# Residual rows of the last group in four parts, and the feed-forward tail's products in another order

## The chip, the core and the metric

The kernel runs on one core of a Trainium2 chip. The core has five engines with a queue each: TensorE (PE in the profile; its weight loads are PEld), VectorE (DVE), ScalarE (ACT), GpSimd (POOL) and SyncE (SP), which here issues most of the DMAs. The metric is the device time of one execution in microseconds (us); the time of a version is the median of its runs.

## What is computed

One decoder layer for 2048 tokens of width 1024 in float32. The reference, cut to what matters here:

```python
a = _rmsnorm(h, g_pre_mix)
u = a @ W_in                       # conv value, conv gate, q, k, v
conv_out = _conformer_conv(...)    # GLU, causal depthwise conv, LayerNorm, swish
attn_out = _stick_breaking(...)    # 8 heads of 64
y = concat(conv_out, attn_out) @ W_out
h = x + _rmsnorm(y, g_post_mix)
f_in = _rmsnorm(h, g_pre_ffn)
f = (silu(f_in @ w_gate) * (f_in @ w_up)) @ w_down      # D_FF = 2816
out = h + _rmsnorm(f, g_post_ffn)
```

## The kernel before

Tokens are worked in four groups of 512 (`g` 0 to 3), each of four row tiles of 128. Float32 matmuls are made of three: each operand is split into a high part `H` (ACT) and a rest `L` (DVE or POOL), and `L*H`, `H*H` and `H*L` are added in PSUM. So every product below is 12 matmuls of 128x128 by 128x512.

The feed-forward part works on two pairs of groups, (0, 1) and (2, 3), and computes gate and up of a pair by seven products in place of eight (a Winograd scheme): the weight matrices and the inputs are cut into 2x2 blocks and summed first. P1 and P2 (function `c11`) and, for the first pair, P4 (function `p4`) are computed earlier, beside attention, and stored in DRAM. Weight sums come from `sums` and lie in DRAM in pairs, two to a tile of 512 KB. The function `part` writes one half of such a tile.

What is left is the stage of the function `five`: 44 blocks, 22 for the first pair of groups, 22 for the second; in each pair of groups 11 column blocks `j`, gate (`i` = 0) and then up (`i` = 1). A block of the first half has the products P5, P7, P6 and P3, one of the second half also P4. PSUM tile `b2` takes P6, then P7 on top (and P4 on top of that); `b3` takes P5, then P3 on top. DVE makes the results of them:

- `u2 = b2 + s1` after P6 (`s1` is P1, loaded; method `second`),
- `u3 = b2 + s1` after P7, then in the first half `p4_ = u3 + p4_`, then `u3 = b3 + u3` after P5,
- `b3 = b3 + u2` after P3.

`result` makes of each of the four the `silu` (gate, on ACT, into a tile of `u`) or the product with the gate's (up, on DVE). After an up block `hidden` makes four sums for the down product (`s1`, `s2`, `a21`, `s4`) and puts the stores of the seven tiles on the list `late`, which `flush` empties two at a time after a product.

Order: products and the sums made through `dve` are kept in the order in which they are written (`tc.keep_in_program_order`). All else (splits, loads, residual rows, input sums) is put by a scheduler that runs when the program is built, and may move as its buffers and inputs allow. The written order in a round of the loop is: P5 of block n; what is left `behind` from block n-1 (a result, `hidden`, and the work of `todo`); P7 of block n; `u3`, `p4_`, `u3`; the split of the first weight pair of block n+1; P6 of block n+1; `u2` of block n+1; P4 of block n (second half); the split of the second weight pair; P3 of block n; `b3`.

`weights` loads for a block: `a22` (tag `row`, 4 buffers) with the stored P4 or a raw weight, the pair (6, 5) in a tile of tag `raw`, and the pair (7, 3) in a tile `raw2` of tag `row`. They are split into `wH` and `wL`, three buffers each.

`todo` gives each block its share of other work, one or two steps of the generator `steps`: first the residual rows of the last group (`residual_parts`, a load `xr` of the row of x, the mean square on ACT with its output in `junk`, `rs` on POOL, a product with the gain on DVE, two adds on POOL, the store to `hd`, a second mean square, a scaling on ACT), then the input sums of the second pair (`input_sums`, transposes of those rows, DVE and POOL sums, stores), then the loads of two of its operands (`operands`). `xr` and `junk` are tiles of tag `row` too. `residual_parts` stops twice; a step does the second part of a row after the first of the next.

The operands are held in slots: `x2` (products 6 and 5 of the first half), `e4`/`e5` (7), `e0`/`e1` (3); `e2`/`e3` get operand 4 of the second half, when the input sums are made. At the end of block 21 operands 7 and 3 are loaded anew for the second half.

After `five` come the down products (in the profile `dps`), in order of product and column block; the change touches them only through the stores of `late`.

## Time and profile before

| | us |
|---|---|
| median of 3 runs | 2599.94 |
| lowest and highest run | 2595.02, 2601.57 |
| the profiled execution, its own time | 2596.21 |
| its span, first to last instruction | 2594.5 |

The mean granted TensorE clock of the profiled execution is 0.977 of full speed. Its stages near the change: the last group's attention and output projection end at 1541.9 us; `five` runs from there to 2151.2; the down products to the end.

In the rows of the profile, L1072 is the line of `dve`, L760 that of the feed-forward matmuls, L1064 and L1065 those of the weight splits, L808 a split of an operand, L1053 the load of a weight pair, L722 the residual's product on DVE, L725 its adds on POOL, L192 the root for `rs`. `b` stands for any PSUM tile of the stage. The buffers of `u2` and `u3` are called `cy`, `cs` and `glu`; `glu` names those of `s1` as well. `accf` is the three sums for down, `a` the tile with `p4_`, `sumf`, `rbf`, `lng` and `accf` are also the tiles of `u`. Of the operands, `xH__17525` is that of P6, `xH__17543` of P5, `e__17561` of P7 and `e__17579` of P3. A row of a timeline gives the start and length in us, the engine, line, operation, what is written from what, the shape, how many in a row, and in brackets how long the engine was idle before and what ended that.

### The profile page before, as it was taken

How to read it: one execution, taken by the hardware profiler on the slowest of the kernel's cores; microseconds unless marked ns; L12 is line 12 of the kernel's file. 1: busy time of each engine (PE TensorE's matmuls, PEld its weight loads, DVE VectorE, ACT ScalarE, POOL GpSimd, SP SyncE). 2: the span in 40 equal slices, each digit the busy share in tenths (PEclk: the TensorE clock that was granted, in tenths of full speed). 3: DMA queues.
4: the chain of work that ended last, by engine and by line, in shares of the span. 5: the costliest groups of instructions: out<-in, count | busy, mean ns of one | idle time of the engine just before them, and what ended most of it. 6: DMA issues, size and time to landing. Idle time of an engine off the chain costs nothing. (4 is left out here: it accounts for less than half of the span.)

```text
span 2594.5 us, 35632 instructions
## 1 busy us (share of the span) xinstructions
PE 2434.6 (94%) x11156; PEld 1963.6 (76%) x11156; DVE 1788.6 (69%) x2321; ACT 1292.8 (50%) x2398; POOL 1473.1 (57%) x1844
## 2 busy tenths in 40 slices
PE   7989989998999999999999988899999999999997
PEld 6877767776777777887788766777777777887886
DVE  5797589958996898876544545766555655557556
ACT  4555555555555656667756734332332233453543
POOL 5764678556755777559433226764443444567556
PEclk9999999999999999999999989999999999999999
DMA  9989888988898898747977636986656557668655
GB/s 341 326 302 310 287 260 279 348 268 284 286 314 272 321 345 280 270 152 235 306 247 235 221 108 220 323 291 223 199 190 201 192 197 262 193 192 283 206 189 174
DMA packets 289182, 657.31 MB, mean 253 GB/s; under 512 B 33889, under 2 KB 42081, under 8 KB 288993
## 3 DMA queue, kind: packets, MB, share of 16 engines
q1 hardware_dynamic: 264704, 622.01, 71.6%
q10 hardware_dynamic: 24288, 33.04, 3.5%
q8 instruction: 88, 1.44, 0.2%
q14 instruction: 102, 0.83, 0.1%
HBM read 460.92 MB, written 193.99 MB: 252 GB/s over the span
## 5 line engine op out<-in xcount | busy, mean ns | idle before, releaser
L573 POOL TENSOR_TENSOR A<-A,om 128x512 f32<-128x512 f32 (+2 forms) x320 | 312.6, 977 | 410.0 <-DVE om L572 372.0
L572 DVE TENSOR_TENSOR_SCAN om<-om,one,z 128x513 f32<-128x513 f32 (+2 forms) x320 | 351.7, 1114 | 110.0 <-ACT A L570 104.5
L1065 POOL TENSOR_TENSOR wL<-raw,wH 128x512 fp32r<-128x512 f32 x176 | 248.9, 1441 | 286.5 <-issue 158.2
L476 DVE SCALAR_TENSOR_TENSOR cv<-glu,cw,cv 128x512 f32<-128x512 f32 x464 | 347.4, 749 | 6.7
L1245 DVE TENSOR_TENSOR xL__21999<-t__22001,xH__21998 128x512 fp32r<-128x512 f32 x154 | 199.1, 1301 | 159.6 <-ACT xH__21998 L1244 159.4
L1243 POOL TENSOR_TENSOR xL__21997<-t__22000,xH__21996 128x512 fp32r<-128x512 f32 x154 | 207.6, 1353 | 175.0 <-ACT xH__21996 L1242 174.5
L256 PE MATMUL inps<-xH,wL 128*128 128x512 f32 x640 | 260.8, 408 | 11.3 <-ACT sg L422 10.3
L249 DVE TENSOR_TENSOR TL<-at,TH 128x512 fp32r<-128x512 f32 (+1 forms) x320 | 188.8, 600 | 112.0 <-ACT TH L248 111.6
L260 PE MATMUL inps<-xL,wH 128*128 128x512 f32 x640 | 258.6, 405 | 0.2 <-DVE xL L392 0.2
L258 PE MATMUL inps<-xH,wH 128*128 128x512 f32 x640 | 258.2, 404 | 0.0
L760 PE MATMUL dps<-xH__21996,xL__21999 128*128 128x512 f32 x616 | 240.9, 391 | 8.1 <-DVE xL__21999 L1245 7.2
L568 ACT ACTIVATE om<-z 128x512 f32<-128x512 f32 (+2 forms) x320 | 171.6, 539 | 153.5 <-PE z L563 70.6
L760 PE MATMUL dps<-xL__21997,xH__21998 128*128 128x512 f32 x616 | 240.8, 391 | 2.0 <-POOL xL__21997 L1243 2.0
L760 PE MATMUL dps<-xH__21996,xH__21998 128*128 128x512 f32 x616 | 240.5, 390 | 0.0
L844 POOL TENSOR_TENSOR sum<-sum 128x512 f32<-128x512 f32 x132 | 172.6, 1308 | 84.8 <-DMA sum<-in_w_up_dram 28.5
L248 ACT ACTIVATE TH<-at 128x512 fp32r<-128x512 f32 (+1 forms) x320 | 168.0, 547 | 103.2 <-PE at L589 94.0
L1242 ACT ACTIVATE xH__21996<-t__22000 128x512 fp32r<-128x512 f32 x154 | 97.2, 631 | 233.0 <-POOL xL__21997 L1243 148.7
L589 PE MATMUL at<-idr,A 128*128 128x128 f32 x1088 | 191.4, 280 | 7.5 <-POOL A L573 5.6
L210 ACT ACTIVATE wH<-raw 128x1024 fp32r<-128x1024 f32 x156 | 165.6, 1064 | 65.0 <-DMA raw<-in_w_in_dram 29.6
L1064 ACT ACTIVATE wH<-raw 128x512 fp32r<-128x512 f32 x176 | 101.1, 623 | 165.0 <-PE b L760 76.4
L570 ACT ACTIVATE A<-z 128x512 f32<-128x512 f32 (+2 forms) x320 | 168.6, 542 | 19.2 <-PE at L589 14.4
L589 PEld LDWEIGHTS at<-idr,A 128*128 128x128 f32 x1088 | 142.2, 144 | 43.9 <-POOL A L573 6.8
(294 smaller groups left out, 6225.8 us busy)
## 6 DMA issues: line engine op xcount, KB each, us to landing
wL<-wL SPq DMA_DIRECT2D x156, 512.0 KB, 5.1
raw<-in_w_in_dram SPq DMA_DIRECT2D x80, 512.0 KB, 6.4
t__22001<-u SPq DMA_DIRECT2D x154, 256.0 KB, 2.8
c<-c ACTq DMA_DIRECT2D x88, 256.0 KB, 4.4
t__22000<-wd SPq DMA_DIRECT2D x88, 256.0 KB, 2.9
K<-kd SPq DMA_DIRECT2D x80, 256.0 KB, 4.7
V<-vd SPq DMA_DIRECT2D x80, 256.0 KB, 4.7
u<-accf SPq DMA_DIRECT2D x22, 768.0 KB, 4.1
```

What stands on the lines that cost most here:

```text
L249: nc.vector.tensor_tensor(L, ps, H.bitcast(F32), ALU.subtract)
L256: nc.tensor.matmul(ps, WL[:, kc], aH[t](k), start=k == 0, stop=False)
L258: nc.tensor.matmul(ps, WH[:, kc], aH[t](k), start=False, stop=False)
L260: nc.tensor.matmul(ps, WH[:, kc], aL[t](k), start=False, stop=k == KT - 1)
L476: nc.vector.scalar_tensor_tensor(to, gl[c][:, k:k + G], cw[:, c, k:k + 1], a, ALU.mult, ALU.add))
L572: nc.vector.tensor_tensor_scan(r, r, z[:, 0:1].to_broadcast([P, w + 1]), one, ALU.mult, ALU.bypass)
L573: nc.gpsimd.tensor_tensor(a[:, 0:w], a[:, 0:w], om[:, G - w + 1:G + 1], ALU.mult)
L589: nc.tensor.transpose(pt[:, j * P:(j + 1) * P], u["A"][j][:, b * P:(b + 1) * P], id32)
L760: return nc.tensor.matmul(ps, a, b, skip_group_check=True, **flags)
L1065: nc.gpsimd.tensor_tensor(l, t, f32(h), sub)
L1243: nc.gpsimd.tensor_tensor(WL, w, f32(WH), sub)
L1245: nc.vector.tensor_tensor(UL, t, f32(UH), sub)
```

## The change

`residual_parts` is given its row and junk tiles. For the last group the rows of x lie in the slots `e2` and `e3`, and the squares go to a tile of tag `ev` (bf16); the other groups use tag `row` as before. It stops three times more finely: after the first mean square, after the adds, after the store with the second mean square, and at the end. A step does one part of up to four rows, the oldest first, so that a row's parts come one block apart. There are seven such steps in place of five, and `todo` gives block 16 two steps.

The weight pairs are (6, 7) and (5, 3), in the stores of `sums` and in `weights`.

In the round of a block P7 comes first and then P5. `u3 = b2 + s1` and the p4 sum are written after P5 as they were after P7. `hidden` stops after two sums: the first two stay in `behind`, with the stores of two tiles, and the other two are made in the next block between the p4 sum and `u3 = b3 + u3`.

```diff
-    def residual(T, keep=False):
-
-        for _ in residual_parts(T, keep):
+    def residual(T):
+
+        for _ in residual_parts(T, row("xr"), row("junk")):
             pass
 
-    def residual_parts(T, keep):
+    def residual_parts(T, r, junk=None, keep=False):
+
         g, t = divmod(T, TT)
         if t == 0:
             gpo.append(gain(g_post_mix))
         y = ys[g][t]
-        r, junk = row("xr"), row("junk")
         nc.sync.dma_start(r, x[T * P:(T + 1) * P, :])
         rs = sp.tile([P, 1], F32, tag="rs", name="rs", bufs=4)
         rms_of(rs, y, junk)
...
             nc.gpsimd.tensor_tensor(y[:, es], y[:, es], r[:, es], ALU.add)
+        yield
         nc.sync.dma_start(hd[T], y)
         rms_of(rstd2[:, T:T + 1], y, junk)
         done.add(("h", T))
+        yield
         if keep:
...
-                    ns = (6, 5) if m in (6, 5) else (7, 3)
+                    ns = (6, 7) if m in (6, 7) else (5, 3)
...
-            for ns in ((6, 5), (7, 3)):
+            for ns in ((6, 7), (5, 3)):
...
             dve(s1, a21, a22, add)
             dve(s2, s1, a11, sub)
+            for n, t in ((1, a11), (4, a22)):
+                late.append([1, t, "u", g, n, j])
+            yield
             dve(a21, a21, a11, sub)
             dve(s4, a12, s2, sub)
-            for n, t in ((1, a11), (4, a22), (7, a21), (2, a12)):
+            for n, t in ((7, a21), (2, a12)):
                 late.append([1, t, "u", g, n, j])
             late.append([1, sums3, "u3", g, j])
+            yield
...
             behind = []
+            more_h = []
             for n in range(NB):
                 b3 = gu("b3")
-                b.mul(b3, 5, True)
+                b.mul(b.b2, 7, False)
                 nxt = Block(n + 1) if n + 1 < NB else None
                 for fn, *args in behind:
                     fn(*args)
                 c11 = result(b.i, (1, 1), b.c11)
-                b.mul(b.b2, 7, False)
+                b.mul(b3, 5, True)
                 u3 = next(u_)
                 dve(u3, b.b2, b.s1, add)
                 p4_ = b.A.get("p4")
                 if p4_ is not None:
                     dve(p4_, u3, p4_, add)
+                if more_h:
+                    next(more_h.pop())
                 dve(u3, b3, u3, add)
...
                 if b.i:
-                    behind.append((hidden, b.g, b.j))
+                    more_h.append(hidden(b.g, b.j))
+                    behind.append((next, more_h[0]))
                 behind += todo.get(n, ())
                 b = nxt
             for fn, *args in behind:
                 fn(*args)
+            next(more_h.pop())
...
-            parts = [residual_parts((NG - 1) * TT + t, True) for t in range(TT)]
-            for t in range(TT + 1):
-                for p in parts[max(t - 1, 0):t + 1][::-1]:
+            xr = [m[:, i:i + 2, :].rearrange("p a t -> p (a t)") for m in operand(*e[2:4], dt=F32) for i in (0, 2)]
+            parts = [residual_parts((NG - 1) * TT + t, xr[t], keep=True) for t in range(TT)]
+            for t in range(TT + 3):
+                for p in parts[max(t - 3, 0):t + 1]:
                     next(p)
                 yield
...
-        todo = {n: [(next, more)] * (1 if n < 5 else 2 - n % 2) for n in range(16)}
+        todo = {n: [(next, more)] * (1 if n < 5 else 2 - n % 2) for n in range(17)}
```

## The prediction

> **What bounds the kernel now.** I read the page first, then a table of windows cut at the stage that the change touches, then what TensorE (PE) waited for in it, then the timelines of the engines that it waited for.
>
> ```profile
> span 2594.5 us, 35632 instructions
> PE 2434.6 (94%) x11156; PEld 1963.6 (76%) x11156; DVE 1788.6 (69%) x2321; ACT 1292.8 (50%) x2398; POOL 1473.1 (57%) x1844
> ```
>
> PE is the bound of the kernel as a whole, so only PE's gaps and its slow stretches can be won. The stage "five" runs from 1541.9 to 2151.2 us. In the table the columns are the window, its length, each engine's busy time with its instructions, the granted clock and the DMA's share and rate.
>
> ```profile
> 1541.90:1639.10 97.20, 85.15 (x353) 66.53 (x351) 58.56 (x70) 41.23 (x68) 61.98 (x55) 0.96 0.70 231
> 1639.10:1720.80 81.70, 72.89 (x305) 57.91 (x305) 58.64 (x69) 25.65 (x46) 56.17 (x40) 0.96 0.90 315
> 1720.80:1826.60 105.80, 100.44 (x421) 79.92 (x422) 61.96 (x74) 34.80 (x62) 54.55 (x40) 0.98 0.71 240
> 1826.60:1853.70 27.10, 22.87 (x85) 17.74 (x84) 17.63 (x23) 9.03 (x16) 12.00 (x9) 0.87 0.67 224
> 1853.70:2136.40 282.70, 282.42 (x1202) 224.92 (x1201) 168.25 (x201) 80.32 (x140) 115.58 (x81) 1.00 0.59 192
> 2136.40:2151.20 14.80, 12.70 (x48) 9.92 (x47) 9.18 (x11) 4.33 (x8) 5.04 (x4) 0.88 0.85 293
> ```
>
> The fifth row is the second half of the stage (blocks of five products): 100 products of 12 matmuls in 282.70 us, PE never idle, clock 1.00. So a product costs **2.83 us** when nothing disturbs it. Against that the other rows lose: 28 products in the first, 97.2 - 79.2 = 18.0 us; 24 in the second, 81.7 - 67.9 = 13.8; 35 in the third, 105.8 - 99.1 = 6.7; 7 in the change of groups, 27.1 - 19.8 = 7.3; 4 at the end, 14.8 - 11.3 = 3.5. That is 49 us, some 2 of it transposes for the input sums. More than this the change cannot give. PE's waits in the first half (1541.9 to 1826.6), total, times and longest:
>
> ```profile
> PE b L760 <- DVE cs L1072: 8.1, 5, 3.4
> PE b L760 <- DVE glu L1072: 7.9, 5, 3.3
> PE b L760 <- DVE cy L1072: 5.5, 3, 1.9
> PE b L760 <- POOL wL L1065: 3.9, 2, 2.7
> ```
>
> `cs`, `glu` and `cy` are the three buffers of `u2` and `u3`. So 21.5 us in 13 waits are for a VectorE (DVE) sum, 3.9 for weights that GpSimd (POOL) had not split. The rest of the loss is matmuls at a lower clock.
>
> **The change part by part.** No instruction is added or dropped: the same products, sums, four row loads of 512 KB and stores; only junk is written in another type. What changes is buffers and order.
>
> *Residual rows.* `xr` and `junk` leave the tag `row` (4 buffers), which then serves the weights alone, two tiles a block. Rows on what that shortage costs now:
>
> ```profile
> 1587.89 3.46 POOL L725 TENSOR_TENSOR big<-big,xr 128x512 f32<-128x512 f32 x2
> ```
> ```profile
> 1591.38 0.32 SPq L1053 DMA_DIRECT2D raw<-S_(7, 3)_8098  x1
> ```
> ```profile
> 1596.27 2.19 ACT L1064 ACTIVATE wH<-raw 128x512 fp32r<-128x512 f32 x4 [8.62 <-DMA raw<-S_(7, 3)_8098]
> ```
> ```profile
> 1598.30 0.50 PE L760 MATMUL b<-e__17561,wL 128*128 128x512 f32 x1 [2.66 <-POOL wL L1065]
> ...
> 1623.13 0.62 PE L760 MATMUL b<-e__17579,wL 128*128 128x512 f32 x1 [1.81 <-DVE cs L1072]
> ...
> 1627.58 0.39 PE L760 MATMUL b<-xH__17543,wL 128*128 128x512 f32 x1
> ```
> ```profile
> 1619.17 1.28 DVE L722 SCALAR_TENSOR_TENSOR big<-big,rs,gain 128x1024 f32<-128x1024 f32 x1 [8.20 <-POOL rs L192]
> ```
>
> POOL's add ends at 1591.35 and frees `xr`; SP issues the weight load 0.03 us later; ScalarE (ACT) has stood 8.62 us for it; PE then waits 2.66. Behind the late split POOL's `rs` is late too, DVE's row product stands 8.20 us at the head of its queue for it, and the `u3` behind that makes PE wait 1.81. The product after that wait took 1627.58 - 1623.13 = 4.45 instead of 2.83: the clock. With buffers of their own and the row product a block after its `rs`, these go: 3.9 of POOL waits, 1.8, and the clock's 4% of 97.2 us (0.96 in the row), 3.9; together 9.6. The four row products (1.28 each) stay in DVE's queue, and one or two will fall into the chain below: **-9 us**. Bounds: 0 (another wait takes over) and -15 (all of the 18.0 but the first block's and one chain's share). The row loads can now go out early on SP, where they wait for nothing.
>
> *The chain from P3 to the next P3.* After a P3 of an up block DVE does nine sums before the next P3 may write `b3`; PE has three products, P5, P7 and the next P6, 8.5 us, to hide them. DVE's rows after the P3 that ended near 1782.1, and POOL beside it:
>
> ```profile
> 1782.28 0.70 DVE L1072 TENSOR_TENSOR b<-b,cy 128x512 f32<-128x512 f32 x1 [0.85 <-PE b L760]
> 1783.08 0.69 DVE L1072 TENSOR_TENSOR lng<-b,lng 128x512 f32<-128x512 f32 x1
> 1783.81 1.07 DVE L1072 TENSOR_TENSOR accf<-lng,sumf 128x512 f32<-128x512 f32 x1
> 1784.91 1.67 DVE L1072 TENSOR_TENSOR accf<-accf,sumf 128x512 f32<-128x512 f32 x1
> 1786.51 1.77 DVE L1072 TENSOR_TENSOR lng<-lng,sumf 128x512 f32<-128x512 f32 x1
> 1788.20 1.77 DVE L1072 TENSOR_TENSOR accf<-sumf,accf 128x512 f32<-128x512 f32 x1
> 1789.90 0.68 DVE L1072 TENSOR_TENSOR cy<-b,glu 128x512 f32<-128x512 f32 x1
> 1791.02 0.69 DVE L1072 TENSOR_TENSOR a<-cy,a 128x512 f32<-128x512 f32 x1 [0.44 <-issue]
> 1791.75 0.69 DVE L1072 TENSOR_TENSOR cy<-b,cy 128x512 f32<-128x512 f32 x1
> ```
> ```profile
> 1783.04 6.39 POOL L1065 TENSOR_TENSOR wL<-raw,wH 128x512 fp32r<-128x512 f32 x4 [5.83 <-ACT wH L1064]
> ```
> ```profile
> 1792.49 0.50 PE L760 MATMUL b<-e__17579,wL 128*128 128x512 f32 x1 [1.89 <-DVE cy L1072]
> ```
>
> PE waits 1.89 because the last of the nine ends at 1792.4. The change keeps all nine: splitting the four sums two and two only puts `u3` and the p4 add (rows seven and eight) ahead of the third and fourth (rows five and six), and swapping P5 and P7 lets `u3` start a product sooner, but DVE is busy with the first sums until 1786.5 in any case. So the gain is in durations: sums that read SBUF alone take 1.67 to 1.77 while POOL splits (to 1789.4) and 0.69 after it. In the new order `u3` runs 1786.5 to 1787.2, the p4 add beside POOL to at most 1788.9, the third sum to some 1789.8, the fourth and the last take 0.7 each: end near 1791.2 instead of 1792.4, 1.2 less. Both ends: 0.69 for all three gives a wait of nothing, 1.9 less; 1.77 for all three gives 1786.5 + 0.7 + 3 x 1.77 + 0.7 = 1793.2, 0.8 more. I take 0.9 less, nearer to the worked order. Of the 13 DVE waits, one is the first block's (1.4) and one the residual's (1.8); the other 11 last 18.3 in all. Eleven times 0.9: 9.9, less 1 for waits shorter than that: **-9**, bounds -18 and +9.
>
> After a P3 of a gate block the chain has no sums for down in it and the swap frees it altogether; its waits (under 0.5) are in the eleven.
>
> *A wait that the swap adds.* P7 accumulates into `b2`, so it must follow `u2`. Two products lay between P6 and P7 (P3, P5), now one. In the first block there is none: P6, then P7.
>
> ```profile
> 1543.64 4.70 DVE L808 TENSOR_TENSOR e__17580<-sumin,e__17579 128x512 fp32r<-128x512 f32 x4 [0.84 <-ACT e__17579 L807]
> ```
> ```profile
> 1549.09 0.47 PE L760 MATMUL b<-e__17561,wL 128*128 128x512 f32 x1 [1.41 <-DVE glu L1072]
> ```
>
> There `u2` is behind four splits until 1548.3. P5 filled that time; now PE stands for all of it, 2.83 more. Queued behind the wait is PE's whole order, which is kept by hand. The longer gap (4.2) will cost the clock too: 4.45 - 2.83 = 1.6 after the 1.81 gap above. **+4.4**, bounds -1.4 (the scheduler puts `u2` ahead of the splits) and +4.5. [...]
>
> *Change of groups and end.* Operand 7 of the first half is read for the last time one product earlier, so its reload and those queued behind it can start 2.8 earlier; PE's wait there ends on POOL, which has this ahead of its weights:
>
> ```profile
> 1836.01 4.68 POOL L808 TENSOR_TENSOR e__19805<-sumin,e__19804 128x512 fp32r<-128x512 f32 x3 [8.71 <-ACT e__19804 L807]
> ```
>
> That start is bound by a load as well, so I take **-2** (0 to -5). In the last block P4 must wait for `u3`:
>
> ```profile
> 2140.72 2.85 DVE L1245 TENSOR_TENSOR xL__21999<-t__22001,xH__21998 128x512 fp32r<-128x512 f32 x2
> ```
> ```profile
> 2144.23 0.72 PE L760 MATMUL b<-e__18237,a22h 128*128 128x512 f32 x2 [2.10 <-DVE glu L1072]
> ```
>
> P7 stood right ahead of P4; now P5 lies between, 2.83 more time: **-2** (0 if `u3` stays behind those splits, -3.5 with the clock). The second half of the stage has P4 as cover (11.3 us for the same nine sums) and stays as it is.
>
> **Sum:** -9 - 9 + 4.4 - 2 - 2 = -17.6. The profiled execution took 2596.2 (span 2594.5 and 1.7 around it), which makes 2578.6. The median of the runs shown is 3.7 above that execution, so I forecast 2582 us.
>
> **Rivals.** *The chain stays (0.17).* Nine sums remain nine, and the moved p4 add now falls beside POOL instead of after it. With all three at 1.7 the chain's term is 0 or worse: -9 + 4.4 - 4 = -8.6 at best, with +0 to +4 for the chain: 2591 to 2595, about 2593. For it: rows three to six are all slow beside POOL. Against it: POOL's work ends, and `u3` reads PSUM at 0.68 within it. [...]
>
> *The rows do not stay apart (0.08).* Only the sums called through `dve` and the products keep their written order; the residual's instructions may move where the scheduler finds room, and stand in front of `u3` as now. The buffers are free all the same: half of the first term, 2587.
>
> *More falls away (0.10).* Waits near 1 us shrink to none, and with them the slow clock (0.96 and 0.98 in the rows): the chain's -18, 2573 or less, to 2565.
>
> *Slower (0.09).* The one mechanism: `u2` too late for P7. The tightest row:
>
> ```profile
> 1681.10 0.68 DVE L1072 TENSOR_TENSOR cs<-b,glu 128x512 f32<-128x512 f32 x1
> ```
> ```profile
> 1682.49 0.39 PE L760 MATMUL b<-xH__17543,wL 128*128 128x512 f32 x1
> ```
>
> `u2` ended at 1681.8, P3 at 1682.5: 0.7 us spare where P7 will now come. It decides from there: if a row product (1.28) or two input sums (0.7 each) more stand ahead of `u2`, each block waits. At 1 us in 22 blocks, +22 + 4.4 - 9 = +17: 2617. Against it: that is the tightest place, and DVE is busy 59 of 97 and 62 of 106 us in the first and third stretch.
>
> **How the numbers follow.** Forecast 0.56, rivals 0.17, 0.08, 0.10 and 0.09. About 0.3% (7.8 us) is what a measurement of this kernel can tell from no change. Faster: 0.56 + 0.08 + 0.10 = 0.74; within: 0.17; slower: 0.09. The range, 2567 to 2601, leaves out the slower rival and the outer halves of two others.
>
> **What would show it.** Right: no weight load behind `xr`, no wait of DVE's row product for `rs`; a first gap near 4 us; the wait before the P3 after an up block about 1 us; the second half as now, 282 to 283 us for its 100 products. Wrong: PE waiting on `u2` ahead of P7 beyond block 0, or the waits before P3 at 1.7 us still.

## The result and the profile after

| | before | changed |
|---|---|---|
| median, with the first measurement (6 runs of each) | 2600.76 us | 2583.57 us |
| ratio, 95% interval | | 0.9934 [0.9916, 0.9952] |
| the profiled execution, its own time | 2596.21 | 2579.23 |
| its span | 2594.5 | 2577.5 |

The changed kernel is faster by 0.66%. The forecast of 2582 us was met within 2 us. The trace shows that it was met partly by chance: the stage won more than the terms said, and the execution lost some of that ahead of the stage.

In the profile after, the line numbers of the code below the residual are two higher: the sums made by `dve` are L1074, the feed-forward matmuls L762, the weight splits L1066 (ACT) and L1067 (POOL). The page opens with

```profile
span 2577.5 us, 35682 instructions
PE 2430.0 (94%) x11156; PEld 1963.3 (76%) x11156; DVE 1793.3 (70%) x2321; ACT 1291.5 (50%) x2398; POOL 1482.5 (58%) x1844
```

The engines do the same work as before (PE 2434.6, DVE 1788.6), so the 17 us of span are waits and slow matmuls. The next view is the changed kernel's table of windows, cut at the same products as in the prediction: the first half, the change of groups (seven products), the 100 products of the second half, the last four, and the tail. Its columns are window, length, busy time and instructions of PE, PEld, DVE, ACT and POOL, granted clock, DMA share and rate.

```profile
1551.00:1815.60 264.60, 253.47 (x1077) 202.03 (x1076) 186.30 (x216) 101.96 (x178) 178.94 (x132) 0.98 0.78 271
1815.60:1840.30 24.70, 20.11 (x85) 15.66 (x84) 16.78 (x19) 7.19 (x13) 15.11 (x10) 1.00 0.70 237
1840.30:2119.90 279.60, 279.60 (x1201) 225.99 (x1200) 162.82 (x200) 80.06 (x140) 115.19 (x81) 1.00 0.59 194
2119.90:2133.60 13.70, 11.42 (x49) 8.96 (x48) 9.25 (x11) 4.52 (x9) 5.35 (x4) 1.00 0.92 306
2133.60:2577.50 443.90, 422.79 (x1849) 347.05 (x1847) 262.45 (x232) 201.77 (x380) 266.08 (x210) 0.99 0.65 213
```

Before, the same stretches took 284.7 (97.2 + 81.7 + 105.8), 27.1, 282.7, 15.1 (up to the first down product) and 443.1. So the first half won 20.1, the change of groups 2.4, the second half 3.1, the end 1.4: 27 us in the stage. But the stage begins at 1551.0 and not at 1541.9, which takes 9.1 back, and the tail 0.8: 17 in all. PE's waits in the first half, in total, times and longest:

```profile
PE b L762 <- POOL ms L191: 4.2, 1, 4.2
PE b L893 <- DVE lnb L914: 2.5, 1, 2.5
PE b L762 <- DVE cy L1074: 1.3, 2, 0.6
PE b L762 <- POOL wL L1067: 1.3, 2, 0.9
PE b L762 <- DVE glu L1074: 1.3, 2, 0.7
PE b L762 <- DVE cs L1074: 0.6, 1, 0.6
```

Waits for the buffers of `u2` and `u3` were 21.5 in 13; three rows hold what is left, 3.2 in five, and all five stand before a P3. Three of them follow an up block. The other two, before the P3 of blocks 13 and 15 (0.61 and 0.63), stand where PE ran P5 of the block ahead of the P3 of the block before, so that only one product lies between P7 and the next P3. So the built program did not keep the written order of the products everywhere. Waits for split weights fell from 3.9 to 1.3. Two rows are new or larger. The first is the gap of block 0: its releaser is given as POOL's `ms`, but the wait is for `u2`, as DVE's timeline shows:

```profile
1552.70 4.66 DVE L810 TENSOR_TENSOR e__17580<-sumin,e__17579 128x512 fp32r<-128x512 f32 x4 [0.83 <-ACT e__17579 L809]
1557.29 0.68 DVE L1074 TENSOR_TENSOR glu<-b,glu 128x512 f32<-128x512 f32 x1
1557.89 1.27 DVE L722 SCALAR_TENSOR_TENSOR big<-big,rs,gain 128x1024 f32<-128x1024 f32 x1
1559.61 2.29 DVE L722 SCALAR_TENSOR_TENSOR big<-big,rs,gain 128x1024 f32<-128x1024 f32 x1 [0.45 <-POOL rs L192]
```

`u2` (second row) ends at 1557.97 behind the four splits, and P7 starts at 1558.11. Rows three and four are two of the residual's row products; all four stand within blocks 0 and 1. The second new wait is of another kind, in PE's timeline:

```profile
1558.11 0.77 PE L762 MATMUL b<-e__17561,wL 128*128 128x512 f32 x1 [4.19 <-POOL ms L191]
...
1620.77 0.65 PE L893 MATMUL b<-idr,big 128*128 128x128 f32 x4 [2.50 <-DVE lnb L914]
...
1623.15 0.63 PE L762 MATMUL b<-e__17580,wH 128*128 128x512 f32 x1
```

L893 is a transpose for the input sums of the second pair, waiting for DVE's sum L914. The P3 behind it runs at 0.63 a matmul and takes 4.45; the granted clock is 0.50 from 1621.99 to 1625.40.

The chain that the prediction worked out row by row can be compared directly. After, in the block at the same place, DVE and then POOL and PE:

```profile
1776.41 1.07 DVE L1074 TENSOR_TENSOR accf<-lng,sumf 128x512 f32<-128x512 f32 x1
1777.52 1.68 DVE L1074 TENSOR_TENSOR accf<-accf,sumf 128x512 f32<-128x512 f32 x1
1779.11 0.68 DVE L1074 TENSOR_TENSOR cy<-b,glu 128x512 f32<-128x512 f32 x1
1779.82 1.06 DVE L1074 TENSOR_TENSOR a<-cy,a 128x512 f32<-128x512 f32 x1
1780.81 1.78 DVE L1074 TENSOR_TENSOR lng<-lng,sumf 128x512 f32<-128x512 f32 x1
1782.52 0.68 DVE L1074 TENSOR_TENSOR accf<-sumf,accf 128x512 f32<-128x512 f32 x1
1783.12 0.68 DVE L1074 TENSOR_TENSOR cy<-b,cy 128x512 f32<-128x512 f32 x1
```
```profile
1775.64 6.40 POOL L1067 TENSOR_TENSOR wL<-raw,wH 128x512 fp32r<-128x512 f32 x4 [5.35 <-ACT wH L1066]
```
```profile
1774.68 0.40 PE L762 MATMUL b<-e__17561,wL 128*128 128x512 f32 x1
...
1783.86 0.50 PE L762 MATMUL b<-e__17579,wL 128*128 128x512 f32 x1 [0.65 <-DVE cy L1074]
```

Two sums for down, `u3`, the p4 add, the other two sums, `u3`: the new order. The third sum falls beside POOL (1.78), the fourth behind it (0.68). From the end of one P3 to the start of the next it takes 9.18 where it was 10.41 (1782.08 to 1792.49). That is 1.23 less; the prediction's worked order gave 1.2.

### The profile page after: what moved, and what is told of

It is laid out like the page before. It is cut to its first block, busy times and chain, and to the rows that moved or that the text cites. A ratio compares the mean times of both kernels' runs of the same rounds, so it can differ in the third digit from the quotient of the medians.

```text
span 2577.5 us, 35682 instructions
## 1 busy us (share of the span) xinstructions
PE 2430.0 (94%) x11156; PEld 1963.3 (76%) x11156; DVE 1793.3 (70%) x2321; ACT 1291.5 (50%) x2398; POOL 1482.5 (58%) x1844
## 4 chain that ended last, share of the span: by engine, by line
PE 52%; DVE 11%; POOL 5%; DMA 4%; issue 3%; ACT 2%; SPq 0%; POOLq 0%; ACTq 0%; DVEq 0%
PE b L762 17%; PE dps L762 13%; PE c L762 8%; DVE cv L476 3%; DVE om L572 2%; PE at L589 2%; PE p L762 1%; PE ops L688 1%; PE ops L689 1%; PE ops L690 1%; PE o L595 1%; PE z L562 1%; PE o L594 1%; PE z L563 1%; DVE TL L249 1%
## 5 line engine op out<-in xcount | busy, mean ns | idle before, releaser
L1067 POOL TENSOR_TENSOR wL<-raw,wH 128x512 fp32r<-128x512 f32 x176 | 255.6, 1478 | 262.9 <-issue 164.6
L762 PE MATMUL dps<-xH__21998,xL__22001 128*128 128x512 f32 x616 | 240.9, 391 | 8.1 <-DVE xL__22001 L1257 7.2
L762 PE MATMUL dps<-xL__21999,xH__22000 128*128 128x512 f32 x616 | 240.6, 391 | 2.2 <-POOL xL__21999 L1255 2.2
L762 PE MATMUL dps<-xH__21998,xH__22000 128*128 128x512 f32 x616 | 240.2, 390 | 0.0
L570 ACT ACTIVATE A<-z 128x512 f32<-128x512 f32 (+2 forms) x320 | 168.4, 542 | 21.0 <-PE at L589 13.6
L1066 ACT ACTIVATE wH<-raw 128x512 fp32r<-128x512 f32 x176 | 101.1, 623 | 154.8 <-PE b L762 77.1
```

Of the source, the lines that this page charges most:

```text
L762: return nc.tensor.matmul(ps, a, b, skip_group_check=True, **flags)
L1067: nc.gpsimd.tensor_tensor(l, t, f32(h), sub)
```

## The experiments

**The theory and its rivals.** By the forecast there are separate terms: row tiles for the weights, a shorter chain, a first block that pays. Against it stand three other readings: the order and the two-and-two sums free the chain only together, so that terms do not add; of the residual part only the buffers count, not the four parts a block apart; and the first gap does not cost its length, since the other engines use the time and the waits move on without it.

Times of the stage below are from the profiles, as in the table above. The changed kernel repeats its stage to 0.2 us (582.6 and 582.8), the kernel before to 3 (609.5 and 606.5). The 0.2 is a lucky pair: the version with operand 3 on DVE and the last version of the table have the same instructions as the changed kernel, in the same order on PE, ACT, POOL and DVE, in the whole first half, and show 266.7 and 263.1 there against 264.6. So a difference of 3 to 4 us in a first half, or 3 in a stage, tells nothing.

An edit can also move what it does not name: the scheduler builds the order of splits, residual rows and input sums anew for each version. Where that bears on a reading, it is said below.

| version | median | ratio to before [95%] | stage | first half | change of groups | 100 products | last four |
|---|---|---|---|---|---|---|---|
| before | 2600.76 | | 609.5 | 284.7 | 27.1 | 282.7 | 15.1 |
| before again | 2600.57 | 1.0003 [0.9984, 1.0022] | 606.5 | 285.2 | 25.0 | 282.7 | 13.6 |
| residual part alone | 2592.88 | 0.997 [0.996, 0.9981] | 604.2 | 279.3 | 26.9 | 282.4 | 15.6 |
| its buffers alone | 2591.1 | 0.9961 [0.9944, 0.9978] | 601.5 | 278.3 | 25.8 | 282.3 | 15.1 |
| order alone | 2599.44 | 0.9987 [0.9974, 1.0] | 604.0 | 280.5 | 26.1 | 282.5 | 14.9 |
| sums alone | 2598.32 | 0.9992 [0.9978, 1.0006] | 606.2 | 285.1 | 25.0 | 280.2 | 15.9 |
| order and sums | 2585.97 | 0.9943 [0.9927, 0.9959] | 594.6 | 272.9 | 26.3 | 279.6 | 15.9 |
| changed | 2583.57 | 0.9934 [0.9916, 0.9952] | 582.6 | 264.6 | 24.7 | 279.6 | 13.7 |
| changed again | 2577.69 | 0.9913 [0.9893, 0.9932] | 582.8 | 264.5 | 24.7 | 279.6 | 13.9 |
| P5 first in block 0 | 2588.46 | 0.9952 [0.9935, 0.9969] | 593.5 | 271.2 | 27.4 | 279.6 | 15.3 |
| that, operand 3 on DVE | 2583.81 | 0.9935 [0.9916, 0.9953] | 587.4 | 272.1 | 21.7 | 279.6 | 14.1 |
| changed, operand 3 on DVE | 2577.42 | 0.9923 [0.9905, 0.994] | 583.4 | 266.7 | 21.7 | 279.6 | 15.4 |
| changed, transposes in other banks | 2584.94 | 0.9941 [0.9924, 0.9957] | 590.6 | 268.4 | 27.4 | 279.6 | 15.2 |
| changed, operand 3 and three splits moved | 2574.77 | 0.9902 [0.9883, 0.9921] | 575.5 | 263.1 | 21.7 | 279.6 | 11.2 |

### One part at a time

**The residual part alone.** From the changed kernel, the products, the pairs and the sums are put back:

```diff
-            for ns in ((6, 7), (5, 3)):
+            for ns in ((6, 5), (7, 3)):
...
-                b.mul(b.b2, 7, False)
+                b.mul(b3, 5, True)
...
-                    more_h.append(hidden(b.g, b.j))
-                    behind.append((next, more_h[0]))
+                    behind.append((hidden, b.g, b.j))
```

> Only the residual part of the change: own tiles for the rows of x and junk, four parts a row; products P5 then P7, pairs (6, 5) and (7, 3), the four sums in one piece as before. The stage (first P6 to first down product) took 609.5 us before and 582.6 after, its first half 284.7 and 264.6. Theory A (three terms that add up: rows about -9, chain about -9 or more, first block about +4): first half 274 to 277, the waits before P3 of 1.5 to 2 us after up blocks still there in every second block, none on POOL's weight splits; time about 0.996 of before. Rival B (the shortage of row tiles is nearly all of it, the chain's waits are only its echo): first half near 265, waits before P3 under 0.7; time 0.993 or less.

The stage took 604.2, the median fell by 8.05 against the kernel before in the same round. Of POOL's late weights one wait of 0.6 is left, but PE waits 22.8 us in 13 times for DVE's `u2` and `u3` (1.4 of it is block 0's, listed under POOL's `ms`), not less than the 21.5 before. The first half, 279.3, is longer than either theory expected.

**The order alone**: P7 ahead of P5, and the pairs; the rest as before.

```diff
-                b.mul(b3, 5, True)
+                b.mul(b.b2, 7, False)
...
-                b.mul(b.b2, 7, False)
+                b.mul(b3, 5, True)
```

> Only the order: P7 ahead of P5, pairs (6, 7) and (5, 3); the four sums in one piece and the residual rows as before. A: first block about 4 to 5 us longer, waits before P3 after up blocks unchanged since DVE still makes nine sums in the old order behind P3, end and change of groups some 2 us shorter each; stage 606 to 611, no change of time that can be told. B: the same stage within 3 us, all of it in the first block. If the order alone frees the chain (DVE starts u3 a product sooner), the waits before P3 fall under 1 us and the first half to 275 or less.

The first half fell by 4.2 to 4.7 although it now holds the gap of 4.2 in block 0; the median moved by 1.5, within its interval.

**The sums alone**: `hidden` in two halves, the second between the p4 add and `u3`.

```diff
+                if more_h:
+                    next(more_h.pop())
                 dve(u3, b3, u3, add)
...
-                    behind.append((hidden, b.g, b.j))
+                    more_h.append(hidden(b.g, b.j))
+                    behind.append((next, more_h[0]))
```

> Only the four sums two and two (third and fourth behind the p4 sum); order P5, P7 and residual rows as before. A: u3 must wait for P7, which ends 5.7 us after P3, when DVE has been through with the first two sums since 4.5, so DVE stands 1.2 us; the sums behind it no longer run beside POOL and cost 0.7 each: end of the chain some 0.5 to 1 us earlier than before, first half 277 to 282. B: nothing, 283 to 286.

The first half stays at 285.1. DVE's timeline of this kernel behind one of the up blocks, and PE's row behind it, show why:

```profile
1715.51 1.67 DVE L1072 TENSOR_TENSOR accf<-accf,sumf 128x512 f32<-128x512 f32 x1
1718.47 0.69 DVE L1072 TENSOR_TENSOR cy<-b,glu 128x512 f32<-128x512 f32 x1 [1.29 <-PE b L760]
1719.20 0.96 DVE L1072 TENSOR_TENSOR a<-cy,a 128x512 f32<-128x512 f32 x1
1720.08 1.77 DVE L1072 TENSOR_TENSOR lng<-lng,sumf 128x512 f32<-128x512 f32 x1
1721.78 1.75 DVE L1072 TENSOR_TENSOR accf<-sumf,accf 128x512 f32<-128x512 f32 x1
```
```profile
1724.18 0.79 PE L760 MATMUL b<-e__17579,wL 128*128 128x512 f32 x1 [2.94 <-DVE cy L1072]
```

After two sums DVE stands 1.29 us, because `u3` needs P7, and P7 is still the second product. The two later sums then come after that pause and PE waits 2.94, where it was 1.85 in the same block before. Behind the last three up blocks the waits are shorter instead, 0.8 for 1.5 to 1.9, and the first half as a whole stands still. Only the second half of the stage wins, 2.5 us.

**Order and sums together**, the residual as before:

```diff
-            xr = [m[:, i:i + 2, :].rearrange("p a t -> p (a t)") for m in operand(*e[2:4], dt=F32) for i in (0, 2)]
-            parts = [residual_parts((NG - 1) * TT + t, xr[t], keep=True) for t in range(TT)]
-            for t in range(TT + 3):
-                for p in parts[max(t - 3, 0):t + 1]:
+            parts = [residual_parts((NG - 1) * TT + t, True) for t in range(TT)]
+            for t in range(TT + 1):
+                for p in parts[max(t - 1, 0):t + 1][::-1]:
```

> Order and sums two and two together, residual rows in tiles of tag row and two parts as before. A: chain about -9 or more, first block +4 to +5, end and change of groups -2 each: first half 277 to 281, stage 599 to 603, time about 0.996 of before; POOL's split waits of blocks 3 to 5 still there. B: stage 607 or more.

The median is 15.0 us less than that of before in the same round, where the two alone gave 1.5 and 2.6. The first half is 12 shorter, more than was expected. With P7 first, `u3` can start as soon as the second sum ends; in one block of this trace it does so at 1693.80, and the two later sums take 0.68 each. So in the first half these two terms do not add; they are one.

**The changed kernel again**, in a later round on another chip, beside the kernel before:

> The whole change once more, unaltered. Its profile began the stage at 1551.0 us against 1541.9 before, with the same instructions on every compute engine up to 1544 us, and its stage was 26.9 shorter, while the median moved by 17.2 only. Scatter theory: the start of the stage lies anywhere in 1540 to 1551 for every version and the stage repeats to 3 us, 580 to 586; then the true gain is near 27 and the median of more runs comes to 2575. Rival: the stage itself scatters by 10 us since a wait of about 2 us may or may not slow the clock; then it comes at 585 to 595 and the median stays near 2583.

2577.69, ratio 0.9913; its stage is the first one's to 0.2. The twelve runs of both have a median of 2580.67, against 2600.91 for all 82 runs of before on record: 20.2 us. The residual part on top of order and sums is then worth 5.3 in the median, with intervals of the ratios that overlap, and 12.0 in the stage: 8.3 in the first half, the rest at the change of groups and the end, where PE's waits differ by 0.6 at most. At the change of groups the clock differs: 0.50 for 3.41 us in the kernel with order and sums (the last section has the rows), 1.00 throughout in the changed kernel. For the end that is not shown.

**The residual's buffers alone**: `xr` and `junk` as in the change, but two parts to a row in the old steps, and the old order and sums.

```diff
-        yield
         nc.sync.dma_start(hd[T], y)
         rms_of(rstd2[:, T:T + 1], y, junk)
         done.add(("h", T))
-        yield
...
-            for t in range(TT + 3):
-                for p in parts[max(t - 3, 0):t + 1]:
+            for t in range(TT + 1):
+                for p in parts[max(t - 1, 0):t + 1][::-1]:
```

> Of the residual part the buffers alone: rows of x in the slots of operand 4, junk in tag ev, but two parts a row in the old steps; order and sums as before. If the shortage of row tiles is what the residual part cures, as the prediction had it, this gives what e1 gave: first half 276 to 282, no split waits in blocks 3 to 5, time 0.996 to 0.998 of before. If the four parts one block apart are what counts (DVE's row product no longer waits for rs at the head of its queue), the first half stays at 283 to 286 and the time at 0.999 to 1.001.

2591.1 against 2592.88 for the whole part. The traces say why they agree: the two are one program, with the same instructions in the same order on all five engines and in the issue of DMAs. The four parts of the source bring nothing, since the scheduler puts the instructions of a row where it did with two, and the stages (604.2 and 601.5) differ by scatter alone. So the buffers are the whole of this part. In the changed kernel, too, the four row products stand in blocks 0 and 1. PE's waits in the first half of this kernel (total, times, longest), whose `dve` line is L1071:

```profile
PE b L759 <- DVE cs L1071: 10.2, 5, 4.7
...
PE b L759 <- POOL wL L1064: 0.6, 1, 0.6
```

The last row is the cure (3.9 before), the first is the price: one wait of 4.7 ahead of an early P3, where 1.2 had stood. With the old chain, DVE takes back part of what the weights give.

### The first gap

The prediction charged 4.4 to a gap of PE in block 0. The edit keeps P5 first in that block alone:

```diff
-                b.mul(b.b2, 7, False)
+                b.mul(*((b.b2, 7, False) if n else (b3, 5, True)))
...
-                b.mul(b3, 5, True)
+                b.mul(*((b3, 5, True) if n else (b.b2, 7, False)))
```

> The whole change, but block 0 keeps P5 ahead of P7, so that P5 fills the time until u2 is written. The first P6 and what follows to the second P6 took 15.5 us in the changed kernel and 10.0 before. If the order costs 4.4 there, as the prediction had it, this gives 10 to 11 us and a stage 4 to 5 us shorter than the changed kernel's, time 0.998 of it. Rival: the wait moves on to block 1 or the input sums (a residual row stands earlier in DVE's queue) and the stage gains 2 us or less.

The gap went back to 1.3, and the stage became 10.9 longer, against every expectation. Of this 6.6 is the first half. The other 4.3 stand at the change of groups and the end, where PE's longest waits are as in the changed kernel (3.01 and 2.35 for 3.02 and 2.28). The changed kernel's granted clock was 1.00 in both places; that it was lower here is my estimate and not shown. PE's waits in the first half:

```profile
PE b L762 <- DVE glu L1074: 5.5, 5, 2.9
PE b L762 <- DVE cy L1074: 4.6, 4, 2.7
PE b L762 <- DVE cs L1074: 3.5, 2, 2.9
PE b L762 <- POOL wL L1067: 3.3, 2, 2.1
```

Three waits of 2.7 to 2.9 for DVE and one of 2.1 for weights stand where the changed kernel has one of 2.5 and none above 0.9 of the other kinds. So taking the gap away did not win its length. Why is not shown. One reading is that a pause of PE at the start is a head start for the other engines, whose residual rows and splits then lie behind them. But the built order changed too: the transposes for the input sums stand behind the 8th to the 24th product of the stage here and behind the 7th to the 20th in the changed kernel, and DVE's four sums `lnb` start 52.6 to 96.7 us into the stage instead of 41.9 to 85.9. The run does not part the two.

**The same with operand 3 split on DVE** at the change of groups, since PE's wait there ends on POOL:

```diff
-        todo[2 * HF - 1] = [(operands, last, [(3, e[0:2])], nc.gpsimd)]
+        todo[2 * HF - 1] = [(operands, last, [(3, e[0:2])])]
```

> As e7, and operand 3 of the second pair is split on VectorE in place of GpSimd. The change of groups took 24.7 us for 7 products (19.8 undisturbed), with 3.0 of wait on GpSimd's weight split behind four splits of operand 3. If that queue is the cause, the wait falls under 1 us and the seven products take 21 to 23 us, 2 to 3 less than e7's. Rival: the operand's load is late in any case (or VectorE's four splits hold back u3), the wait stays at 2 to 3 us under another name and the seven take 24 to 26.

The change of groups fell from 27.4 to 21.7; the wait of 3.0 for POOL's weights is gone. The first half did not move beyond scatter (272.1).

**The changed kernel with that one edit:**

> The whole change with operand 3 of the second pair split on VectorE in place of GpSimd, the first block as changed. In e8 this took the seven products at the change of groups to 21.7 us against 27.4 in e7 and 24.7 in the changed kernel. If that gain is its own: first half as in the changed kernel (264.5), seven products 21.5 to 22, stage 579 to 580.5 against 582.7, time 0.990 to 0.992 of before. Rival: the built order of the first half changes too, as in e7, and the first half comes at 270 or more.

The change of groups is 21.7 again, 3.0 less, but the first half is 2.1 and the end 1.7 longer: the one wait for `lnb` grew from 2.5 to 3.8, and the last block's P4 waited 2.4 and took 4.33 in place of 2.89. In the first half the order is that of the changed kernel, and before that P4 PE waits no longer than there (2.28 and 2.51), so neither is shown to be the edit's doing. The stage as a whole stands still (583.4). Against this kernel the version above, with P5 first in block 0, is 5.4 longer in the first half and 4.0 in the stage, which is the fairer price of that edit.

### The new wait for the input sums

PE's transposes (L893) use a tile of tag `bank`. If that buffer holds them, one of the six of `gu` frees them:

```diff
-                yield from input_sums(last, k, tmp, bank, B[last][4])
+                yield from input_sums(last, k, tmp, gu, B[last][4])
```

> The whole change with the transposes of the input sums in the six-buffer PSUM tag of b2 and b3 in place of the two-buffer tag. In the changed kernel PE stands 2.5 us before a transpose (until VectorE's lnb has read the bank) and P3 of block 4 is slowed to 4.45: about 5 us in all. If the two banks are the cause, that wait and the slow P3 go, first half 259 to 262, stage about 578. Rival: VectorE's queue is the cause, the bank only where it shows; then PE waits for b2 or b3 or for u3 instead, first half 264 to 270.

The wait on `lnb` is gone from the list of PE's waits in the first half, but its first row is now

```profile
PE b L762 <- DVE glu L1074: 7.8, 3, 4.0
```

and the first half is 3.8 longer, at the edge of the scatter. The edit did more than change the buffer. The scheduler put the transposes behind the 28th to the 60th product, and `lnb` runs 89.6 to 189.1 us into the stage. So it is not shown whether the wait of 2.5 is one for a buffer or for DVE's time; what is shown is that with the input sums at this later place PE waits 4.0 and 3.1 for DVE sums.

### The end, and the shortest stage

In the last block `u3` stands behind splits for the down products on DVE, as before the change. Three of them go to POOL, with operand 3 on DVE as above:

```diff
-            nc.vector.tensor_tensor(UL, t, f32(UH), sub)
+            (nc.gpsimd if (g, n) == (0, 1) and j in (1, 2, 3) else nc.vector).tensor_tensor(UL, t, f32(UH), sub)
```

> As e9, and the rests of the down product's loads 1 to 3 are split on GpSimd in place of VectorE, so that u3 of the last block stands behind one such split alone. The last four products took 13.7 to 13.9 us in the changed kernel with 2.3 to 2.5 of wait on u3. If those splits are the cause: 11.5 to 12.5 us, stage 2 us below e9's. Rival: GpSimd's eight splits delay the first down products, the wait only moves there: first to last the same.

The last four products take 11.2, which is four times 2.8, the change of groups 21.7, the stage 575.5. DVE's `u3` of that block:

```profile
2118.18 0.69 DVE L1074 TENSOR_TENSOR glu<-b,glu 128x512 f32<-128x512 f32 x1 [0.90 <-PE b L762]
```

Now DVE waits for PE's P7 and not PE for DVE. This version has the shortest stage, by 7.1, of which 1.5 lies in the first half, where nothing was edited. Its median of 2574.77 us is 5.9 below the pooled one of the changed kernel, but the intervals of the ratios overlap (0.9902 [0.9883, 0.9921] and 0.9913 [0.9893, 0.9932]). Its tail took 449.5, where the changed kernel's two profiles had 443.9 and 449.3, so whether the splits on POOL cost something there is not settled.

### What stood ahead of the stage

The changed kernel's stage begins later (1551.0 and 1548.3) than that of before, while its code ahead of the stage is the same but for the loads of the residual rows, which now go out early. The kernel before, unaltered, was run for a second start:

> The kernel before, unaltered, for a second profile. Scatter theory: its stage repeats (608 to 611 us, first half 283 to 286) and its start may lie anywhere in 1540 to 1551. Rival: the changed kernels start later by their nature, some 6 us, and give that much of the stage's gain back; then this starts in 1540 to 1544 like the five other profiles that lack one of the order and the sums. A start of 1546 or more speaks for scatter, one in 1540 to 1544 leaves the rival open.

It began at 1543.3. The six profiles without both of order and sums begin at 1540.4 to 1543.4, the eight with both at 1542.7 to 1551.0. The groups overlap in one profile only, and the tail varies by 6 us as well (443.1 to 449.5). Two things in the traces speak for scatter. The kernel with the order alone and the one with order and sums have the same instructions in the same order ahead of the stage on PE, DVE, POOL and SP, and begin at 1540.4 and 1549.7. And 8.4 of the changed kernel's 9.1 had come about at 1020 us, long before the residual's loads go out at 1516.8, which are thus not the cause. Whether some 5 us are given back ahead of the stage by a cause in the change, as the stage's 25.3 (mean of two profiles each) against the medians' 20.2 suggests, stays open.

## Why the prediction was right, point by point

**The number.** The sum was -17.6 in the profile's own time and the profile moved by 17.0. Of this the stage is -26.9 (-23.8 against the second profile of before), its later start +9.1, the tail +0.8. The terms undersold the stage by 9 us, and what no term spoke of took as much back. The forecast was right in its sign and its main mechanisms, and in its number by two errors that met.

**Residual rows, -9 (0 to -15).** The size is borne out: on top of order and sums the first half fell by 8.3 and the stage by 12.0. The cause was half right. The shortage of row tiles is the cause (the buffers alone are the whole part); "the row product a block after its `rs`" is not: the products stand in blocks 0 and 1, and DVE still waits there for `rs`, 4.2 in three where it was 19.3 in four. The sign "no wait of DVE's row product for `rs`" did not come. The rival "the rows do not stay apart" was right as a mechanism, and wrong in its price of half the term. Nor is the gain free-standing: alone it is 5 to 7 in the first half, since DVE's waits stay at 22.8.

**The chain, -9 (-18 to +9).** This is the mis-sized term. Its waits fell from 18.3 to 3.2, 15.1. Not all of it is the chain's own: with order and sums alone 8.6 is left, and the rest needs the residual part. The worked block was right to 0.03 us in its sum, with two errors in it that met: the p4 add took 1.06 and not up to 1.7, the third sum 1.78 and not 0.9. And it was one block, in which POOL's four splits start just behind P3. I multiplied its gain by eleven. Before the P3 of blocks 6 to 12, where the waits were longest (to 3.4), nothing is left. The second, third and fourth sum of such a block after, and POOL beside them:

```profile
1662.40 1.67 DVE L1074 TENSOR_TENSOR accf<-accf 128x512 f32<-128x512 f32 x1
...
1665.69 0.68 DVE L1074 TENSOR_TENSOR sumf<-sumf,accf 128x512 f32<-128x512 f32 x1
1666.29 0.68 DVE L1074 TENSOR_TENSOR accf<-sumf,accf 128x512 f32<-128x512 f32 x1
```
```profile
1660.43 3.09 POOL L1067 TENSOR_TENSOR wL<-raw,wH 128x512 fp32r<-128x512 f32 x2 [0.75 <-ACT wH L1066]
1663.47 1.75 POOL L810 TENSOR_TENSOR t__19404<-sumin,t__19403 128x512 fp32r<-128x512 f32 x1
```

POOL is through at 1665.2, and both later sums take 0.68. The step that failed is "eleven times 0.9": what stands on POOL beside the sums differs from block to block. The text also valued the sums' split and the swap by what DVE is busy with; the run with the sums alone, where DVE stands 1.29 for P7, shows a block in which the split needs the swap. And the text had the chain freed altogether behind gate blocks; two waits of 0.6 stand there, where the built order has P5 ahead of P3.

**The first block, +4.4 (to +4.5).** From its first P6 to the next it took 15.5, before 10.0: +5.4, of it 2.8 the gap, as worked out, and 2.6 slow matmuls (0.63 in place of 0.40, at a granted clock of 0.50 from 1557.14 to 1563.96), forecast as 1.6. As a price of the order it is not borne out: the version without the gap was longer, not 4.4 shorter, by 5.4 to 6.6 in the first half. A wait was charged as though it stood alone, and so was the built order, which changed with it; what the gap alone costs stays open.

**Change of groups, -2 (0 to -5).** 2.4 against one profile of before, 0.3 against the other. The reload's earlier start is not shown to matter; the bound is POOL's queue, as the operand on DVE shows (-3.0).

**The end, -2 (0 to -3.5).** The bound of 0 came about, by the condition named with it: `u3` stayed behind the splits, and PE waits 2.3 where it was 2.1. The 1.4 won against the first profile of before go with the granted clock, 0.88 there and 1.00 after; against the second there is nothing.

**The second half, "as now, 282 to 283".** Wrong: 279.6. In the trace of before, one block in two has a P4 that starts late. DVE's and PE's rows of one, with the last matmul ahead of the P4:

```profile
1873.83 1.78 DVE L1072 TENSOR_TENSOR accf<-sumf,accf 128x512 f32<-128x512 f32 x1
1875.53 0.68 DVE L1072 TENSOR_TENSOR cy<-b,glu 128x512 f32<-128x512 f32 x1
```
```profile
1875.88 0.39 PE L760 MATMUL b<-t__19404,wH 128*128 128x512 f32 x1
1876.27 0.73 PE L760 MATMUL b<-e__18237,a22h 128*128 128x512 f32 x2
```

`u3` ends at 1876.21 behind the fourth sum, and P4 starts 0.16 after its turn (0.23 from matmul to matmul). In ten of twenty blocks the product ahead of P4 so takes 2.96 or a little more and P4 itself 2.88, with 2.80 for the others: some 2.7 us. Such delays are too small for a list of waits, and I had taken 2.83, the mean with them in it, for an undisturbed product. The sums alone bring 2.5 of the 3.1, the order alone 0.2.

**The other rivals.** "The chain stays" fell, though its mechanism is there: the p4 add took 1.06 beside POOL in place of 0.69. Within the same 6.40 us of POOL the sums of two SBUF tiles took 1.06 to 1.78 and `u3`, with one of its inputs in PSUM, 0.68; so the stretch of such a sum there is 1.1 at most. "More falls away" named what happened to the chain (15 of 18), and the start hid it. "`u2` too late for P7" did not occur beyond block 0: no other wait of a P7 for `u2` stands in the changed kernel's first half (one of 1.0, in block 1, stands in that of the version with operand 3 on DVE). Not foreseen was the wait of the transposes for `lnb`, 2.5, and some 1.6 more in the P3 behind it, which took 4.45 with the granted clock at 0.50 for 3.41 of it.

## What to carry to other kernels

Work out a gain for each place where the wait occurs, with what the neighbouring engine does there; one block times the number of blocks was off by two thirds. Two edits to one chain can be worth next to nothing alone and 15 us together, when one gives work a place and the other makes its input come in time. Taking away a wait at the head of a stage need not win its length: try it in a run before counting it as a loss. And where a scheduler builds the order, compare the built orders of two versions before reading their times: here two versions were one program, and two small edits moved the input sums as well.

## What the runs showed of the hardware

The length of PE's pause alone did not decide here whether the clock dropped. At the change of groups PE stands 3.02 before the same product in the changed kernel and in the one with order and sums alone:

```profile
1831.82 0.50 PE L762 MATMUL b<-t__19403,wL 128*128 128x512 f32 x1 [3.02 <-POOL wL L1067]
```
```profile
1838.83 0.50 PE L760 MATMUL b<-t__19401,wL 128*128 128x512 f32 x1 [3.02 <-POOL wL L1065]
```

The same pause costs nothing more in one, and in the other the granted clock is 0.50 from 1.5 us on (a matmul of that product then takes 0.63 in place of 0.40, and the product 4.05). Pauses of 1.81 and 2.50 were followed by slow matmuls as well (0.62 and 0.63 in the rows above). What goes with it can be read from the clock records of the traces. In the profiled executions of the kernel before and of the changed one the granted clock is 1.00 or 0.50, and all its changes lie 3.41 us or a multiple of it apart (50 and 44 records). Windows cut on that grid of 3.41 us show the two cases (columns as in the tables of windows), first the changed kernel and then the other:

```profile
1826.79:1830.20 3.41, 2.01 (x9) 1.30 (x7) 3.41 (x4) 1.15 (x2) 3.41 (x3) 1.00 0.24 93
1830.20:1833.61 3.41, 1.79 (x8) 1.47 (x9) 1.04 (x2) 0.63 (x1) 3.41 (x3) 1.00 0.66 265
```
```profile
1836.90:1840.31 3.41, 1.49 (x6) 1.24 (x7) 1.35 (x2) 0.63 (x1) 3.41 (x4) 1.00 0.75 300
1840.31:1843.72 3.41, 3.41 (x9) 2.64 (x8) 0.60 (x1) 0.00 (x0) 2.18 (x2) 0.50 0.48 169
```

In the first the pause is shared by two stretches of the grid, with PE busy for 2.01 and 1.79; in the second most of it falls into one, PE is busy for 1.49, and the next stretch has a granted clock of 0.50. In the stages of the kernel before and of the changed one this parts every case: of 337 stretches at 1.00, the 9 that were followed by 0.50 had PE busy for 0.20 to 1.53 us, and the 328 others for 1.57 at least. Over the whole of the two executions it does not: stretches with up to 2.17 were followed by 0.50, and one with 1.55 was not. So 1.5 us is no limit that these traces show; why the clock drops is not shown either.

The part of the execution ahead of the stage, with the same instructions in almost the same order on the engines, took 1540.4 to 1551.0 us in the fourteen profiles, while 100 products of the second half took 279.6 in eight of them, to 0.1.
